# Where the sums for the output projection are made: from beside the second half of the input projection to beside the last six blocks of its first half

## The chip, the core and the metric

The kernel runs on one core of a Trainium2 chip. A core has five engines with one queue each: TensorE (PE, matrix products; PEld is its loading of stationary operands), VectorE (DVE), ScalarE (ACT), GpSimd (POOL) and SyncE (SP), which here issues nearly all transfers between the chip's memory and the core's own. The metric is the device time of one execution in microseconds. The kernel before takes 2552.73 us, the median of three runs (2552.61 to 2555.01).

## The reference

One layer of a streaming encoder on x, 2048 tokens by 1024, in fp32. Only the first part matters here:

```python
u = rms_norm(h, g_mix_pre[l])
z = u @ w_in[l]                                   # 1024 x 2816
qa, ka, va, qh, fh, ih, gh = jnp.split(z, IN_SPLITS, axis=-1)
ya = swa_with_sinks(...)                          # banded attention on qa, ka, va
yh = hgrn2(...)                                   # gated recurrence on qh, fh, ih, gh
y = jnp.concatenate([ya, yh.astype(ya.dtype)], axis=-1) @ w_out[l]    # 1024 x 1024
h = h + rms_norm(y, g_mix_post[l])
...                                               # cross-attention, then a SwiGLU FFN
```

## The kernel before

Every fp32 matrix product is made of three products in a shorter format (fp32r): an operand is split into a high part (ScalarE or GpSimd) and the rest (VectorE, the subtraction at L990).

*Blocks of seven.* Most large products use Strassen's scheme in Winograd's form. An operand is a 2 by 2 arrangement of quarters, and a product of two of them takes seven products of quarters instead of eight, at the price of sums of quarters on both sides. The stationary operand's sums are made block by block (`streamed`, L1065, whose tiles are `sraw`, `sum` and `S`). The moving operand has four sums, under the keys 5, 7, 6 and 4 (CHAIN, L992). Where the moving operand is a weight, its sums are made ahead: `combined` (L1027) loads quarters, adds or subtracts them on VectorE (L1034) and stores the results in the chip's memory. `sums` (L1418) sets aside that memory, `out_s` for the output projection's w_out, and returns a function that starts the generator `combined`. Each sum is made in two halves of 128 partitions by 1024 numbers (512 KB): eight operations, twelve quarter loads and eight stores in all. The job for the output projection reads `out_s` much later, at 778 us.

`phases` (L1219) walks through jobs of such blocks. A block of kind "s" has seven steps (STEPS, L980), each of twelve matrix products. After each step every generator in the list `after` is moved on once: the closing work of earlier blocks, and what a job's last entry names, a table from the index of a block to generators that begin at it.

*The first half of the input projection* (`in_first`, L451) is one such job over tokens 0 to 1023, with thirteen blocks: the first four are the plain halves of the first two column pairs, then come nine of kind "s", one for each further pair of column groups (ORDER, L419). The moving operand is the normalised input, the stationary one w_in. A block's results are added (L644), copied or passed through a tanh, and stored in z_d. The blocks with index 5 to 8 hold gate and query columns of the recurrence: their closing work makes the decays (`decays`, L726: logarithm, scan at L734, exponentials, with small GpSimd operations between) beside the block that follows. Also beside these blocks the second half's input is normalised, transposed (L1398) and stored. The job's table is empty, `{}`.

*The second half* (`mix`, L194) projects tokens 1024 to 2047 column by column (`in_proj`, plain products at L156 to L158) between the banded attention (`swa`, iterations with L805 to L853) and the recurrence (`hgrn`). After nine iterations the loop over the remaining eight attention iterations moves the sums' generator on by four steps each, and by one before it. There the sums use the tiles `u` (two buffers) and `x` (three buffers), which they share with the decays of this half:

```python
self.out_sums, side = self.sums("out_s", self.w_out, 4, lambda: self.io_tile("u"), lambda: self.io_tile("x"))
side = side()
next(side)
pairs = self.hgrn(range(NPB, NT), "gt")
for i, _ in enumerate(swa, NPB + 2):
    next(cols)
    ...
    for _ in range(4):
        next(side, None)
```

*What sets the order.* A planner at build time sets each engine's order: it takes instructions by the order in which the program states them, each as soon as it is ready in the planner's own reckoning of times, and it derives all waits. `behind` (L1050) keeps an operation on VectorE or ScalarE behind the last one stated before a mark, which `phases` sets after the products of each step. A tile with n buffers can be filled again when the last reader of its oldest use is done.

## Time and profile before

| what | value |
|---|---|
| median of three runs | 2552.73 us |
| the profiled execution | 2550.01 us, span 2548.3 us |
| TensorE busy | 2504.8 us (98%) |
| VectorE busy | 1792.1 us (70%) |
| ScalarE busy | 1261.6 us (50%) |
| GpSimd busy | 364.6 us (14%) |
| granted TensorE clock, mean | 0.997 |
| the eight sums (L1034 with `u` and `x`) | 448 to 524 us |
| moved by DMA | 486.33 MB, 191 GB/s over the span |

In the lines of the profile, "out<-in" names the tile that an instruction writes and those that it reads, and L with a number is the line of the kernel. A line of the order of time gives start, duration, engine, line, operation, tiles and count, and in square brackets how long the engine idled before it and what ended that. A line of the busy time by stretches gives, after the two ends of the stretch in us, its length and the busy time of PE, PEld, DVE, ACT and POOL with the number of instructions in brackets, the granted clock, the mean busy share of the 16 DMA engines, and GB/s. A line of waits gives the waiting instruction, what it waited for, the total in us, how often, and the longest. A queue's name ends in q (SPq). Products overlap in the engine, so that a product's own duration (0.39 us) is longer than the distance to the next (0.23 us).

### The profile page before, as it was taken

What the parts mean: (1) busy time and instruction counts of PE and PEld (TensorE: products, weight loads), DVE (VectorE), ACT (ScalarE), POOL (GpSimd) and SP (SyncE); (2) the same over time, 40 slices, a digit from 0 to 9 for tenths busy, and PEclk for the clock granted to TensorE, in tenths of its full rate; (3) what the DMA queues carried; (4) which work ended last, traced back from release to release, by engine and by line L of the source; (5) the groups of instructions that cost most, each with busy time, mean ns of one, the idle gap of its engine ahead of it and who ended that gap; (6) DMA issues with size and microseconds to landing.
All of it is one profiled execution on the core that took longest, in us unless ns stands there. A gap on an engine that the chain in (4) does not pass through costs nothing.

```text
span 2548.3 us, 34324 instructions
## 1 busy us (share of the span) xinstructions
PE 2504.8 (98%) x12006; PEld 2092.8 (82%) x12006; DVE 1792.1 (70%) x2871; ACT 1261.6 (50%) x2635; POOL 364.6 (14%) x540
## 2 busy tenths in 40 slices
PE   9999999999999999999999999999999999999998
PEld 8878888877997778878878888888888888878886
DVE  8885488987556989988876555576566557574766
ACT  5553466655555566566753333353333335443543
POOL 4231234321311112102200000000000000000022
PEclk9999999999999999999999999999999999999999
DMA  6455655865887996867954522254465434564786
GB/s 201 146 165 178 192 154 170 230 204 146 259 292 275 316 335 189 274 206 226 333 200 146 177 91 87 74 203 148 160 210 195 144 117 159 180 188 106 228 177 151
DMA packets 387885, 486.33 MB, mean 191 GB/s; under 512 B 22272, under 2 KB 283392, under 8 KB 387712
## 3 DMA queue, kind: packets, MB, share of 16 engines
q1 hardware_dynamic: 381664, 462.12, 55.9%
q0 software_dynamic: 6048, 22.02, 5.0%
q8 instruction: 94, 1.54, 0.2%
q14 instruction: 79, 0.65, 0.1%
HBM read 317.34 MB, written 166.72 MB: 190 GB/s over the span
## 4 chain that ended last, share of the span: by engine, by line
PE 51%; DVE 2%; DMA 1%; issue 1%; ACT 1%; POOL 0%; SPq 0%; DVEq 0%; POOLq 0%; ACTq 0%
PE psm L1133 17%; PE psm L1131 17%; PE psm L1132 17%; DVE T L990 0%; DVE S L990 0%; ACT junk L1504 0%; PE pss L1390 0%; DMA out_dram<-row 0%; DMA row<-d_s 0%; DMA row<-in_w_down_dram 0%; DMA u_d<-row 0%; DMA sraw<-in_w_gate_dram 0%; DVE sum L1106 0%; ACT S L987 0%; ACT T L987 0%
## 5 line engine op out<-in xcount | busy, mean ns | idle before, releaser
L1131 PE MATMUL psm<-T,S 128*128 128x512 f32 x2680 | 1034.1, 390 | 13.3 <-ACT part L1146 7.2
L1132 PE MATMUL psm<-T,S 128*128 128x512 f32 x2680 | 1042.3, 390 | 4.0 <-DVE T L990 3.9
L1133 PE MATMUL psm<-T,S 128*128 128x512 f32 x2680 | 1029.4, 389 | 4.1 <-DVE S L990 4.1
L1131 PEld LDWEIGHTS psm<-T,S 128*128 128x128 f32 x2680 | 503.0, 188 | 125.9 <-ACT part L1146 11.9
L1132 PEld LDWEIGHTS psm<-T,S 128*128 128x128 f32 x2680 | 503.2, 188 | 110.5 <-DVE T L990 7.3
L1133 PEld LDWEIGHTS psm<-T,S 128*128 128x128 f32 x2680 | 503.1, 188 | 110.6 <-DVE S L990 6.3
L987 ACT ACTIVATE S<-sum 128x512 fp32r<-128x512 f32 (+1 forms) x370 | 224.0, 620 | 371.5 <-PE psm L1133 267.3
L990 DVE TENSOR_TENSOR S<-sraw,S 128x512 fp32r<-128x512 f32 (+1 forms) x315 | 211.5, 679 | 218.8 <-ACT S L987 215.8
L1146 ACT ACTIVATE part<-psm 128x512 f32<-128x512 f32 x285 | 168.6, 596 | 251.9 <-PE psm L1133 230.9
L990 DVE TENSOR_TENSOR S<-sum,S 128x512 fp32r<-128x512 f32 (+1 forms) x388 | 257.4, 673 | 42.1 <-ACT S L987 38.3
L987 ACT ACTIVATE S<-sraw 128x512 fp32r<-128x512 f32 (+1 forms) x300 | 184.7, 618 | 110.8 <-PE psm L1133 106.0
L1537 POOL DMA_DIRECT2D y_d<-row x16 | 14.1, 879 | 1077.9 <-DVE row L1721 1027.6
L990 DVE TENSOR_TENSOR T<-row,T 128x1024 fp32r<-128x1024 f32 (+1 forms) x112 | 131.0, 1183 | 30.2 <-ACT T L987 29.2
L157 PE MATMUL psg<-u,whi 128*128 128x512 f32 x320 | 128.3, 401 | 0.0
L158 PE MATMUL psg<-u,wlo 128*128 128x512 f32 x320 | 127.6, 399 | 0.0
L156 PE MATMUL psg<-u,whi 128*128 128x512 f32 x320 | 127.5, 399 | 0.0
L1504 ACT ACTIVATE junk<-row 128x512 f32<-128x512 f32 x160 | 99.6, 624 | 40.6 <-DVE row L1526 20.6
L987 ACT ACTIVATE T<-row 128x1024 fp32r<-128x1024 f32 (+1 forms) x112 | 113.3, 1031 | 7.5 <-DMA row<-d_s 4.3
L1672 DVE TENSOR_TENSOR row<-psm,part 128x512 f32<-128x512 f32 x66 | 43.7, 687 | 66.9 <-PE psm L1133 66.9
L1681 DVE TENSOR_TENSOR part<-psm,part 128x512 f32<-128x512 f32 x66 | 43.8, 687 | 60.1 <-PE psm L1133 59.8
L1721 DVE TENSOR_TENSOR row<-psm,part 128x512 f32<-128x512 f32 x72 | 49.1, 688 | 49.5 <-PE psm L1133 49.4
L814 ACT ACTIVATE S<-S,w_mn 128x256 f32<-128x256 f32 (+1 forms) x128 | 63.0, 496 | 29.6 <-DVE w_mn L810 29.2
(363 smaller groups left out, 3562.2 us busy)
## 6 DMA issues: line engine op xcount, KB each, us to landing
sraw<-in_w_gate_dram SPq DMA_DIRECT2D x44, 512.0 KB, 3.6
sraw<-in_w_up_dram SPq DMA_DIRECT2D x44, 512.0 KB, 3.7
hid_d<-row SPq DMA_DIRECT2D x44, 512.0 KB, 2.7
sraw<-hid_d SPq DMA_DIRECT2D x32, 512.0 KB, 4.2
sraw<-in_w_in_dram SPq DMA_DIRECT2D x44, 256.0 KB, 4.0
z_d<-pair SPq DMA_DIRECT2D x20, 512.0 KB, 3.4
raw<-in_w_in_dram SPq DMA_DIRECT2D x20, 512.0 KB, 4.8
z_d<-z SPq DMA_DIRECT2D x20, 512.0 KB, 4.0
```

The source lines that it names most:

```text
L156: nc.tensor.matmul(ps, ah, bh, start=(i == 0), stop=False)
L157: nc.tensor.matmul(ps, ah, bl, start=False, stop=False)
L158: nc.tensor.matmul(ps, al, bh, start=False, stop=(i == n - 1))
L814: nc.scalar.activation(s[:, r, o:], s[:, r, o:], AF.Exp, bias=mn[:, i:i + 1], scale=-1.0, accum_out=den[:, i:i + 1])
L987: self.nc.scalar.activation(hi, raw, AF.Copy)
L990: self.nc.vector.tensor_tensor(lo, raw, f32(hi), ALU.subtract)
L1131: nc.tensor.matmul(ps, s[:, 0, k, :], t[:, 0, k, :], start=st, stop=False, **kw)
L1132: nc.tensor.matmul(ps, s[:, 0, k, :], t[:, 1, k, :], start=False, stop=False, **kw)
L1133: nc.tensor.matmul(ps, s[:, 1, k, :], t[:, 0, k, :], start=False, stop=sp, **kw)
L1146: nc.scalar.activation(t, ps, AF.Copy)
L1504: self.nc.scalar.activation(junk, a, AF.Square, scale=float(D) ** -0.5, accum_out=to)
L1721: nc.vector.tensor_tensor(d, a, b, ALU.add)
```

## The change

The sums of w_out for the output projection are made earlier: their generator starts at the block with index 7 of the first half's job, the eighth, and moves on once per step of the last six blocks (42 steps). It uses two tiles of its own with one buffer each, `wa` and `wb`, in the pool of that stage (`st_pool`). With `late=True` a sum is stored at the step after the one in which it is made, so that a sum takes five moves of the generator: loads, two empty ones, the operation, the store. The later loop no longer moves the sums on. For the sums that the later jobs make, `late` is False and `put` does what it did.

```diff
@@ mix
-                self.out_sums, side = self.sums("out_s", self.w_out, 4, lambda: self.io_tile("u"), lambda: self.io_tile("x"))
-                side = side()
-                next(side)
                 pairs = self.hgrn(range(NPB, NT), "gt")
                 for i, _ in enumerate(swa, NPB + 2):
                     next(cols)
                     if i == NT + 1 - 0:
                         next(pairs)
-                    for _ in range(4):
-                        next(side, None)
@@ in_first
-        phases = self.phases([(lambda i, j, a, n: raw[i, j][:, a:a + n, :], 4, blocks, None, {})], T)
+        def weight_tile(tag):
+            self._n += 1
+            return self.st_pool.tile([P, D], F32, tag=tag, name=f"{tag}_{self._n}", bufs=1)
+
+        self.out_sums, side = self.sums("out_s", self.w_out, 4, lambda: weight_tile("wa"), lambda: weight_tile("wb"),
+                                        late=True)
+        phases = self.phases([(lambda i, j, a, n: raw[i, j][:, a:a + n, :], 4, blocks, None, {7: [side]})], T)
@@ combined
-    def combined(self, get, nk, dst):
+    def combined(self, get, nk, dst, late=False):
...
                 with self.behind():
                     nc.vector.tensor_tensor(t, t, o, op)
+                if late:
+                    yield
                 self.store(dst[self.CHAIN.index(key), :, a * 512:b * 512], t.rearrange("p k d -> p (k d)"))
...
-                    put(4, o, t, ALU.subtract)
+                    yield from put(4, o, t, ALU.subtract)
                 else:
-                    put(key, t, o, ALU.add if key == 6 else ALU.subtract)
+                    yield from put(key, t, o, ALU.add if key == 6 else ALU.subtract)
                 yield
@@ sums
-    def sums(self, name, src, nk, *tiles):
+    def sums(self, name, src, nk, *tiles, late=False):
...
-        return dst, lambda: self.combined(get, nk, dst)
+        return dst, lambda: self.combined(get, nk, dst, late)
```

## The prediction

> **What bounds the kernel now.** I read the page first, then the busy time by stretches of 25 us over the two stages that the change touches, then what TensorE waited for in them, and last the order of time on VectorE and on the DMA queue.
>
> ```profile
> PE 2504.8 (98%) x12006; PEld 2092.8 (82%) x12006; DVE 1792.1 (70%) x2871; ACT 1261.6 (50%) x2635; POOL 364.6 (14%) x540
> ```
>
> TensorE is busy for 2504.8 of 2548.3 us, so all its idle time together is 43.5 us. The change removes no matmul. It can only move this idle time, and 0.2% of the time is 5.1 us. The stretches say where it lies.
>
> ```profile
> core 0: us, PE busy (x) PEld busy (x) DVE busy (x) ACT busy (x) POOL busy (x), PEclk, DMA share, GB/s
> 100.00:125.00 25.00, 24.50 (x108) 19.97 (x107) 22.74 (x31) 15.61 (x25) 10.50 (x13) 1.00 0.41 127
> 125.00:150.00 25.00, 22.85 (x100) 18.29 (x99) 23.71 (x31) 17.31 (x26) 11.50 (x13) 1.00 0.48 143
> 150.00:175.00 25.00, 24.05 (x106) 19.58 (x105) 23.66 (x32) 13.50 (x22) 11.59 (x14) 1.00 0.50 152
> 175.00:200.00 25.00, 25.00 (x112) 20.70 (x111) 14.88 (x23) 8.26 (x15) 2.69 (x5) 1.00 0.69 226
> 200.00:225.00 25.00, 25.00 (x112) 20.69 (x111) 15.29 (x23) 8.42 (x14) 2.76 (x4) 1.00 0.50 174
> 275.00:300.00 25.00, 23.85 (x124) 19.91 (x123) 17.91 (x57) 12.95 (x45) 7.80 (x13) 0.93 0.75 203
> 475.00:500.00 25.00, 24.90 (x138) 20.95 (x136) 23.43 (x45) 16.60 (x46) 8.81 (x14) 1.00 1.08 289
> 500.00:525.00 25.00, 23.83 (x124) 19.42 (x123) 21.72 (x54) 13.53 (x38) 7.39 (x9) 1.00 1.04 321
> 525.00:550.00 25.00, 24.27 (x122) 19.60 (x122) 21.80 (x62) 13.94 (x43) 8.04 (x13) 1.00 0.61 189
> 625.00:650.00 25.00, 22.27 (x170) 21.16 (x168) 18.15 (x25) 15.38 (x31) 4.65 (x7) 0.93 0.95 256
> ```
>
> The sums now run in the stage from 445 to 525 us, where VectorE is busy 87 to 94% and TensorE idles 0.10, 1.17 and 0.73 us in the three stretches shown. The first half of the input projection is two stages in one: up to 175 us VectorE is busy 23.7 of 25 us and TensorE loses 0.50, 2.15 and 0.95 us; from 175 us VectorE has 10 us of each 25 to spare and TensorE loses nothing.
>
> Where block eight begins follows from the decays, which are made beside the block after theirs. Their eight scans are four pairs on VectorE from 106.10 to 167.98 us, beside the blocks with index 6, 7, 8 and 9, so one of these blocks takes 61.88/3, 20.6 us. Block eight (index 7) begins near 125 us, index 8 near 146, index 9 near 166, and the last ends near 246.
>
> ```profile
> L734 DVE TENSOR_TENSOR_SCAN pair<-reset,pair x8: 1192/1208/1562, 106.1 to 169.1; 128x512 f32<-128x512 f32 x8
> PE psm L1131 <- ACT part L1146: 4.1, 5, 1.2
> 148.99 0.50 PE L1131 MATMUL psm<-T,S 128*128 128x512 f32 x1 [1.20 <-ACT part L1146]
> 157.66 1.48 DVE L672 SCALAR_TENSOR_TENSOR pair<-pair,pair 128x512 f32<-128x512 f32 x2 [0.31 <-ACT pair L749]
> 159.83 1.22 DVE L754 SCALAR_TENSOR_TENSOR pair<-pair,pair 128x1024 f32<-128x1024 f32 x1 [0.69 <-ACT pair L750]
> 160.97 1.28 DVE L644 TENSOR_TENSOR pair<-psm,part 128x512 f32<-128x512 f32 x2
> 162.17 0.68 DVE L990 TENSOR_TENSOR S<-sum,S 128x512 fp32r<-128x512 f32 x1
> 167.41 0.64 DVE L990 TENSOR_TENSOR S<-sum,S 128x512 fp32r<-128x512 f32 x1
> 167.98 1.21 DVE L734 TENSOR_TENSOR_SCAN pair<-reset,pair 128x512 f32<-128x512 f32 x1
> ```
>
> In these blocks TensorE waits once a block, about 1.2 us, for a copy on ScalarE that releases a bank. That copy stands behind the decays' logarithm, which stands behind what VectorE delivers at 160.97. VectorE works without a gap from there to the next scan, and its only idle time in the loop is 0.31 and 0.69 us. So the loop from scan to scan is VectorE's, and what is put into it lengthens the block.
>
> **The change part by part.** *The operations that move.* Eight sums leave the later stage and come into the first half, at these prices now:
>
> ```profile
> L1034 DVE TENSOR_TENSOR u<-u,x x6: 1198/1214/1224, 448.1 to 521.9; 128x1024 f32<-128x1024 f32 x6
> L1034 DVE TENSOR_TENSOR x<-x,u x2: 1206/1216/1225, 494.4 to 523.6; 128x1024 f32<-128x1024 f32 x2
>   DMA out_s<-u: 2.8, 1
>   issue: 0.3, 1
> 521.91 1.22 DVE L1034 TENSOR_TENSOR u<-u,x 128x1024 f32<-128x1024 f32 x1 [2.76 <-DMA out_s<-u]
> 523.05 0.68 DVE L853 TENSOR_TENSOR ys<-psh,ys 64x512 f32<-64x512 f32 x1
> PE psh L805 <- DVE ys L853: 0.7, 1, 0.7
> ```
>
> One is 1.21 us, all eight 9.7 us. In the new place a sum takes five steps of the generator: loads, two idle steps, the operation at the fourth, the store at the fifth. The generator moves once per step, seven steps a block, 42 steps in the six blocks from index 7; 41 are needed, so all fit. The operations fall on steps 4, 9, 14, 19, 24, 29, 34 and 39. That is one in block index 7, two in index 8, and five in index 9 to 12.
>
> *Cost of the three early operations.* The first comes just ahead of the row at L672, where VectorE idles 0.31 us: it costs 1.21 less 0.31, 0.9 us. The second comes between the scan and what follows it, with no gap: 1.2 us. The third comes at the end of index 8, ahead of the scan at 168 us. It delays that, but the block after it is the last with decays, and TensorE waits for nothing in 175 to 225 us: between 0 and 1.2, I take 0.6. Sum 2.7 us, bounds 0.9 (first alone counts) and 3.6 (three in full).
>
> *Cost of the five late operations.* Nothing: 5 times 1.21 is 6.1 us over some 75 us in which VectorE idles 10 of every 25. If that cover were gone they would cost up to 6.1.
>
> *Waits of these operations for their data.* In the stage before, eight operations waited 2.8 and 0.3 us, 0.38 each on average, and TensorE felt it: the 2.76 us wait held L853, and TensorE waited 0.7 us for L853. Behind a sum that waits now stand the additions at L644, the decays and the splits, whose readers are ScalarE and TensorE. For the three early ones I take 3 times 0.38, 1.1 us; bounds 0 and 3 times 2.76, 8.3 us. The five late ones wait in VectorE's spare time.
>
> *The DMA queue.* SP receives 20 load commands for twelve tiles (those of the upper half of rows are two commands each) and eight stores, in a stage where the DMA share is 0.41 to 0.69; it loses them in a stage at 1.04 to 1.08. The tiles are now one buffer each. So three loads (steps 6, 21 and 26) wait for the landing of the store issued one step earlier, and the third and seventh operations for a store four steps earlier.
>
> ```profile
> L78 SPq DMA_DIRECT2D out_s<-u x6: 326/334/543, 449.3 to 523.2; - x6
> L78 SPq DMA_DIRECT2D out_s<-x x2: 320/429/538, 496.8 to 524.9; - x2
> DMA to landing us min/median/max: 2.6/6.0/10.9
> 198.62 0.92 SPq L75 DMA_DIRECT2D sraw<-in_w_in_dram  x2
> 208.90 0.68 DVE L1106 TENSOR_TENSOR sum<-sraw,sraw 128x512 f32<-128x512 f32 x1
> sraw<-in_w_in_dram SPq DMA_DIRECT2D x44, 256.0 KB, 4.0
> ```
>
> The landing line covers all accesses of the sums' array (eight stores and eight later loads), median 6.0 us. A step is 20.6/7, 2.9 us. So SP stands about 3.1 us at each such load, and behind it stand the weight loads of the next block (sraw), loads of x and stores of z. These have cover: the weights issued at 198.62 land about 4.0 us later and are first read at 208.90, 6.3 us to spare. I take 0 for it. If the cover is gone it is at most 3 times 3.1, 9.3 us.
>
> The Trainium skill, DMA: Bandwidth & Descriptors, section on the anatomy of a DMA, fits a transfer by 2.0 us plus its bytes over 436 GB/s, for the software path. By it 512 KB would land in about 3.2 us (an estimate), SP would stand 0.3 us instead of 3.1, and the sum would be the same, with 0.9 in place of 9.3 as its far end. The row's median of 6.0 us comes from a stage with a full DMA, so the true one may lie between.
>
> *What the later stage gains.* VectorE loses 9.7 us of work and 3.1 us of waits between 445 and 525 us. TensorE's idle time there is the upper bound on the gain: 0.10 plus 1.17, and 0.73 more until 550 us if the lag is carried on. Below it is 0. I take 1.3 us, since these waits, with the one for L853 above, are for VectorE:
>
> ```profile
> PE pss L839 <- DVE w_mn L810: 0.5, 1, 0.5
> PE psh L849 <- DVE ptl L844: 0.3, 1, 0.3
> ```
>
> *Hand-over between the stages.* Two tiles of 4 KB per partition are added to the pool of the first half, and the next stage's tiles come to lie elsewhere. The stretch 275 to 300 us has the granted clock at 0.93, 7% of 25 us or 1.7 us. A shift of the work may add one such stretch or remove one; I take 0, ends minus 1.7 and 1.7.
>
> *Sum.* 2.7 + 1.1 - 1.3 = +2.5 us on the profiled execution's 2550.0 us (span 2548.3), so 2552.5. That execution is 2.7 us under the median of the runs, 2552.73; on the median the forecast is 2555.2 us, 0.10% slower, which lies inside the 0.2% (5.1 us) that a measurement of this kernel can tell from no change.
>
> **The rivals.** *Slower: the sums wait in VectorE's full stretch.* The mechanism is the wait of 2.76 us above, now at all three early operations. For it: the buffers are single, and the loads for a sum are issued only three steps (8.7 us) ahead, with SP standing up to 3.1 us of that. Against it: VectorE lags there, which gives the loads time. It gives 2.7 + 8.3 - 1.3, +9.7 us, 2562.4. It decides the sign of the measurement once the waits exceed 3.7 us in total (2.7 + 3.7 - 1.3 = 5.1), which is two of three.
>
> The Trainium skill, TensorE: Matmul & The Clock Gate, part 1, says that the clock falls to half after an idle window of about 3.4 us; a stall of that length would add about 1.7 us to this rival, by an estimate from the page. This trace has the clock at 0.93 in 275 to 300 us with 1.15 us of idle time in the whole stretch, so less idle time is enough here.
>
> *Slower: SP's queue holds the weights.* A load that stands for the landing of a store holds the next block's weights past the 6.3 us of cover, and the stationary operands are late. It needs landings near the 10.9 maximum: 10.9 - 2.9 - 6.3, 1.7 us of stall each, at three places 5.1 us; +7.6 us with the sum above, 2560.3.
>
> *Faster.* The later stage is freed of more than its own waits: all 2.0 us of 475 to 550, and the hand-over in 625 to 650 us with its 2.73 us idle and 1.7 us of low clock, while only the first early operation costs its 0.9: -5.5 us, 2547.2. For it speaks that VectorE is full up to 550 us. Against it: the last sum ends at 525, and the longest wait of the hand-over is for a load.
>
> ```profile
> PE pst L902 <- DMA v<-z_d: 2.6, 1, 2.6
> ```
>
> **How the numbers follow.** I give the forecast (2555.2, within 0.2%) 0.48, the slower rivals 0.30 and 0.08, the faster one 0.14. The likeliest case's own range is 2550 to 2558: the ends 0.9 - 2.0 - 1.7 = -2.8 and +5.1. The range for all reaches to the faster rival's 2547 and just past the slower ones' 2562.4, to 2563; about 2 in 10 is left out, most of it waits with a low clock on top and gains beyond the rival's. Faster 0.14, same 0.48, slower 0.38.
>
> **What would show it.** Right: the sums' rows on VectorE stand near 135, 150, 165 us and later, each 1.2 us; TensorE's wait for the copy at L1146 near 149 and 168 us grows from 1.2 to about 2 us; from 175 to 246 us TensorE idles as little as now; the whole first half ends 2 to 4 us later; the idle time of the stretches from 475 to 525 us (shifted by as much) falls below 0.3 us. Wrong: a wait for a landing ahead of a sum of over 1 us at two places (the slower rival), splits waiting for sraw (the second), scans still 20.6 us apart in spite of the sums (then the loop has slack that I don't see), or a later stage that becomes shorter by more than 2 us.

## The result and the profile after

The kernel after takes 2563.07 us, the median of six runs (2561.36 to 2565.05), beside 2552.85 us for the kernel before in the same comparison (2552.24 to 2555.01). That is 10.2 us more, a ratio of 1.004 with a 95% interval of 1.003 to 1.005. In a second comparison the ratio was 1.003 (1.0015 to 1.0045). The change makes the kernel slower by 0.3 to 0.4%. The forecast was +0.10%, and the end of the range, 2563, was just missed.

In the kernel after, lines 238 to 535 have numbers smaller by five, and those from 537 on numbers larger by one to three: the products are L1134 to L1136 (before L1131 to L1133), the copy that releases a bank L1149 (L1146), the addition L645 (L644), the scan L735 (L734), the sums L1035 (L1034).

Line of the page on the busy time of the engines, kernel after (span 2561.5 us, the execution itself 2563.24 us):

```profile
PE 2508.2 (98%) x12006; PEld 2098.1 (82%) x12006; DVE 1794.0 (70%) x2871; ACT 1260.1 (49%) x2635; POOL 363.3 (14%) x540
```

The work is the same, so the time is TensorE's idle time and its clock. Busy time by stretches, kernel before and then kernel after (columns: the stretch, its length, PE, PEld, DVE, ACT, POOL with their instructions, granted clock, DMA share, GB/s):

```profile
25.00:50.00 25.00, 24.88 (x136) 21.18 (x136) 23.75 (x33) 12.97 (x25) 14.94 (x17) 1.00 0.51 151
100.00:250.00 150.00, 145.91 (x638) 119.19 (x637) 116.40 (x159) 75.00 (x116) 42.38 (x54) 1.00 0.50 157
475.00:550.00 75.00, 73.00 (x381) 59.96 (x380) 66.94 (x159) 44.07 (x126) 24.23 (x35) 1.00 0.91 266
600.00:700.00 100.00, 94.74 (x686) 88.23 (x685) 57.22 (x96) 53.67 (x135) 24.99 (x34) 0.98 0.74 217
```

```profile
25.00:50.00 25.00, 21.63 (x120) 18.00 (x119) 18.84 (x27) 10.53 (x22) 14.97 (x17) 1.00 0.63 148
100.00:250.00 150.00, 142.44 (x622) 116.03 (x621) 123.87 (x163) 76.11 (x118) 46.60 (x55) 1.00 0.68 217
475.00:550.00 75.00, 74.30 (x401) 62.71 (x399) 66.81 (x173) 47.32 (x135) 24.83 (x38) 1.00 0.48 153
600.00:700.00 100.00, 92.77 (x636) 86.56 (x637) 50.74 (x78) 46.35 (x112) 20.53 (x27) 0.95 0.72 213
```

The two kernels differ at four places. TensorE loses 3.25 us more between 25 and 50 us, a place that the prediction does not speak of. It loses 3.5 us more between 100 and 250 us. Between 475 and 550 us it loses 1.3 us less. Between 600 and 700 us it is busy 2 us less and its clock is 0.95 instead of 0.98, worth another 3 us of work; the prediction has this place only in its faster rival, as a gain.

Since the stretches shift against each other, the exact account is made at equal work: the products in TensorE's order are given their undisturbed spacing (0.227 us for 512 columns and so on), and two traces are compared by the time at which the same sum of spacings is reached. This lag is my working from the start times of the 12006 products; the spacing taken for the smaller products moves a term by up to 0.6 us. The table gives what each stretch (named by the times of the kernel before) adds to the lag behind the profiled execution before, in us. Each row is one execution of the kernel named. The last column is the difference of the medians.

| kernel | to 57 | 57–272 | 272–316 | 316–479 | 479–563 | 563–625 | 625–672 | 672–941 | rest | sum | medians |
|---|---|---|---|---|---|---|---|---|---|---|---|
| after | +3.8 | +4.1 | −2.6 | −0.1 | −2.8 | −0.1 | +5.7 | +3.2 | +2.1 | +13.2 | +10.2 |
| after_again | +4.3 | +4.6 | −2.1 | +0.4 | −2.8 | −0.1 | +4.0 | +6.6 | −0.8 | +14.1 | +8.9 |
| before_again | −0.5 | +0.9 | 0.0 | +0.1 | +0.1 | 0.0 | −1.3 | +0.7 | +1.1 | +1.2 | |
| early_loads_alone | +3.2 | +1.8 | −2.3 | +0.3 | −0.7 | 0.0 | +1.5 | +2.3 | +1.4 | +7.5 | +2.7 |
| held_loads | −0.5 | +9.5 | −2.3 | +0.1 | −2.8 | −0.1 | +3.5 | +1.9 | +0.1 | +9.3 | +9.7 |
| held_behind_x | −0.2 | +8.1 | −2.0 | +0.8 | −2.8 | −0.1 | +4.6 | +7.4 | +2.8 | +18.5 | +9.8 |
| small_ops | −0.1 | +5.8 | −2.8 | +1.1 | −2.8 | −0.1 | +2.9 | +5.4 | −1.3 | +7.9 | +3.6 |
| from_nine | 0.0 | +5.8 | +4.2 | +0.3 | −2.8 | −0.1 | +3.3 | +3.8 | −0.4 | +14.1 | +8.8 |
| not_late | +5.2 | +8.7 | −2.2 | +0.8 | −2.8 | −0.2 | +4.0 | +6.1 | +0.5 | +20.2 | +10.2 |
| held_next | +4.9 | +2.8 | −1.8 | +0.3 | −2.8 | +0.5 | +5.5 | +2.0 | +0.4 | +11.9 | +7.7 |
| both | +3.8 | +4.4 | −0.3 | +0.8 | +1.9 | 0.0 | −0.3 | +3.2 | +9.2 | +22.8 | +17.0 |
| in_fold | −0.1 | −0.1 | −2.1 | +0.8 | −2.7 | −0.1 | +8.0 | +3.4 | −1.0 | +6.0 | +2.1 |
| old_late | −0.4 | +0.3 | −2.6 | 0.0 | −0.1 | 0.0 | −0.1 | +4.3 | +3.1 | +4.5 | −0.7 |
| first_nine | −0.3 | +0.3 | +5.2 | +5.7 | −4.0 | +1.0 | +2.5 | +3.1 | −0.9 | +12.6 | +8.7 |
| spread | −0.3 | −0.3 | +4.0 | +4.2 | −2.1 | −0.3 | +5.0 | +4.7 | −0.1 | +14.8 | +7.3 |

The profiled execution before is 2.7 us under its median, which is why most sums lie above the differences of the medians. The stretches 272 to 316, 672 to 941 and the rest vary by several us between kernels that are alike there: old_late, whose median is that of the kernel before, has −2.6, +4.3 and +3.1 in them. So nothing is read from these three in the kernel after. The other terms are +3.8, +4.1, −0.1, −2.8, −0.1 and +5.7, together +10.6 us against +10.2 measured; the three left out add up to +2.7, as much as the execution before lay under its median, a match that may be chance.

**The start.** Order of time on the queue of SP, kernel after:

```profile
18.14 1.71 SPq L75 DMA_DIRECT2D wa<-in_w_out_dram  x2
19.89 0.61 SPq L75 DMA_DIRECT2D wb<-in_w_out_dram  x1
21.02 3.41 SPq L75 DMA_DIRECT2D sraw<-in_w_in_dram  x2
24.47 0.61 SPq L75 DMA_DIRECT2D wb<-in_w_out_dram  x1
25.18 4.61 SPq L75 DMA_DIRECT2D sraw<-in_w_in_dram  x4
```

The loads of the first two quarters (four commands, 1 MB) are stated at the block with index 7, near 125 us, but they are issued at 18 us. They depend on nothing, their tiles are free from the start, and the planner takes each instruction as soon as it is ready. In the kernel before eight loads of the first weights (sraw) stand at that place:

```profile
18.26 9.86 SPq L75 DMA_DIRECT2D sraw<-in_w_in_dram  x8
```

Now they come later, and the DMA share from 25 to 50 us is 0.63 instead of 0.51. Who waited on GpSimd between 18 and 50 us, before and then after (total, times, longest in us):

```profile
POOL S_u L989 <- DMA sraw<-in_w_in_dram: 0.8, 1, 0.8
```

```profile
POOL S_u L990 <- DMA sraw<-in_w_in_dram: 5.3, 3, 4.3
```

In the same stretch, from 25 to 50 us, TensorE waited 3.4 us in the kernel after, 2.1 of them for a split on VectorE (L991); in the kernel before it idles 0.1 us there.

**The first half.** Waits of TensorE from 100 to 250 us, kernel after (total, times, longest in us):

```profile
PE psm L1134 <- ACT part L1149: 6.7, 5, 2.0
PE psm L1134 <- DVE pair L645: 0.8, 1, 0.8
```

One line of its order of time there:

```profile
154.95 0.50 PE L1134 MATMUL psm<-T,S 128*128 128x512 f32 x1 [2.05 <-ACT part L1149]
```

The wait for the copy is the one of before (4.1 us in five), grown by 2.6 us. Of this growth 1.0 us stands at 113 and 134 us, ahead of the first sum, and after_again does not have it. The other 1.7 us stands at 155 and 176 us, where the first two sums are in VectorE's order: 2.05 and 1.78 us, where the kernel before has 1.20 and 0.95 (after_again 1.92 and 1.67). The order of time on VectorE, kernel after, the three early sums and the sixth with the addition behind it:

```profile
140.40 1.22 DVE L1035 TENSOR_TENSOR wa<-wa,wb 128x1024 f32<-128x1024 f32 x1
153.08 1.59 DVE L1035 TENSOR_TENSOR wa<-wa,wb 128x1024 f32<-128x1024 f32 x1
178.17 1.21 DVE L1035 TENSOR_TENSOR wa<-wa,wb 128x1024 f32<-128x1024 f32 x1
210.01 1.23 DVE L1035 TENSOR_TENSOR wa<-wa,wb 128x1024 f32<-128x1024 f32 x1 [6.23 <-DMA wa<-in_w_out_dram]
211.16 1.28 DVE L645 TENSOR_TENSOR pair<-psm,part 128x512 f32<-128x512 f32 x2
```

The scans stand as one group (first and last start):

```profile
L735 DVE TENSOR_TENSOR_SCAN pair<-reset,pair x8: 1192/1210/1560, 111.1 to 175.5; 128x512 f32<-128x512 f32 x8
```

From the first scan to the last it is now 64.4 us, where it was 63.0. The early sums have no bracket: they waited for nothing. The third came at 178 us, behind the last scan and not ahead of it. The one at 210 us waited 6.2 us for its load, and the addition L645 stood behind it, for which TensorE then waited 0.8 us (2.8 in after_again). The queue of SP shows why that load was late: its tile has one buffer, so it went out only when the store of the sum before, in the same tile, had landed (3.3 us after its issue), and it then took 6.6 us itself.

```profile
200.08 0.32 SPq L78 DMA_DIRECT2D out_s<-wa  x1
203.44 0.37 SPq L75 DMA_DIRECT2D wa<-in_w_out_dram  x1
```

**The hand-over.** Waits of TensorE from 610 to 680 us, kernel after; before, the longest was the one for a load of `v` in the prediction:

```profile
PE pst L926 <- ACT vt L905: 4.5, 2, 2.5
PE psg L887 <- DVE z L714: 2.4, 1, 2.4
```

ScalarE's order of time shows what stood in front. The splits of the output projection's first operands (`T<-z`) waited there for their loads, and the copies for which TensorE waited stood behind them: the last column's `z` at 631.11 us, and `vt`.

```profile
629.20 1.06 ACT L988 ACTIVATE T<-z 128x1024 fp32r<-128x1024 f32 x1 [5.90 <-DMA z<-in_w_out_dram]
636.50 1.06 ACT L988 ACTIVATE T<-z 128x1024 fp32r<-128x1024 f32 x1 [2.86 <-DMA z<-in_w_out_dram]
637.46 0.58 ACT L905 ACTIVATE vt<-pst 128x512 f32<-128x512 f32 x1
```

first_nine and, but for held_next, all executions with the sums in the first half alone have these two waits, 3.2 to 5.5 us for `vt` and 1.8 to 2.6 us for `z`. Part of the loss is clock. The granted clock is at half for 10.2 us in this stretch of the kernel after, for 3.4 us in after_again and in the kernel before, and not at all in before_again. So 3.4 of the +5.7 us in the table are clock in the one execution, and none of the +4.0 in the other.

### The profile page after: what moved, and what is told of

It is laid out like the page before. It is cut to its first block, busy times and chain, and to the rows that moved or that the text cites. A ratio compares the mean times of both kernels' runs of the same rounds, so it can differ in the third digit from the quotient of the medians.

```text
span 2561.5 us, 34342 instructions
## 1 busy us (share of the span) xinstructions
PE 2508.2 (98%) x12006; PEld 2098.1 (82%) x12006; DVE 1794.0 (70%) x2871; ACT 1260.1 (49%) x2635; POOL 363.3 (14%) x540
## 4 chain that ended last, share of the span: by engine, by line
PE 57%; DVE 3%; DMA 3%; issue 1%; ACT 1%; SPq 0%; POOL 0%; DVEq 0%; POOLq 0%; ACTq 0%
PE psm L1136 19%; PE psm L1135 19%; PE psm L1134 19%; DVE T L991 1%; DVE S L991 1%; DMA sraw<-in_w_gate_dram 0%; ACT junk L1507 0%; PE pss L1393 0%; DVE sum L1109 0%; DMA row<-qk_s 0%; DVE row L1401 0%; DMA h1t_d<-row 0%; DMA row<-qk_d 0%; DMA row<-in_w_down_dram 0%; DMA row<-vo_s 0%
## 5 line engine op out<-in xcount | busy, mean ns | idle before, releaser
L1134 PE MATMUL psm<-T,S 128*128 128x512 f32 x2680 | 1035.8, 391 | 18.3 <-ACT part L1149 10.0
L1136 PE MATMUL psm<-T,S 128*128 128x512 f32 x2680 | 1032.2, 391 | 4.4 <-DVE S L991 4.2
L1134 PEld LDWEIGHTS psm<-T,S 128*128 128x128 f32 x2680 | 504.0, 188 | 131.2 <-ACT part L1149 14.7
L1136 PEld LDWEIGHTS psm<-T,S 128*128 128x128 f32 x2680 | 504.4, 188 | 111.4 <-DVE S L991 7.3
L991 DVE TENSOR_TENSOR S<-sraw,S 128x512 fp32r<-128x512 f32 (+1 forms) x315 | 211.9, 682 | 208.2 <-ACT S L988 206.6
L1149 ACT ACTIVATE part<-psm 128x512 f32<-128x512 f32 x285 | 168.6, 596 | 252.1 <-PE psm L1136 231.5
L991 DVE TENSOR_TENSOR S<-sum,S 128x512 fp32r<-128x512 f32 (+1 forms) x388 | 259.9, 681 | 40.7 <-ACT S L988 38.7
L991 DVE TENSOR_TENSOR T<-row,T 128x1024 fp32r<-128x1024 f32 (+1 forms) x112 | 131.3, 1186 | 30.6 <-ACT T L988 28.6
L1109 DVE TENSOR_TENSOR sum<-sraw,sraw 128x512 f32<-128x512 f32 (+1 forms) x97 | 66.3, 683 | 15.9 <-issue 9.3
```

The lines of the kernel that those rows point to most:

```text
L991: self.nc.vector.tensor_tensor(lo, raw, f32(hi), ALU.subtract)
L1109: nc.vector.tensor_tensor(t, a, b, op)
L1134: nc.tensor.matmul(ps, s[:, 0, k, :], t[:, 0, k, :], start=st, stop=False, **kw)
L1136: nc.tensor.matmul(ps, s[:, 1, k, :], t[:, 0, k, :], start=False, stop=sp, **kw)
L1149: nc.scalar.activation(t, ps, AF.Copy)
```

## The experiments

**Only the early loads.** To the kernel before, a generator at the block with index 7 adds the loads of the first two quarters into `wa` and `wb`, which nothing reads; the sums stay in the second half.

```diff
+        def fetched():
+            for tag, i, j in (("wa", 0, 1), ("wb", 0, 0)):
...
+                self.w_out(t.rearrange("p (k d) -> p k d", d=512), i, j, 0, 2)
+            yield
-        ... blocks, None, {})], T)
+        ... blocks, None, {7: [fetched]})], T)
```

> The kernel before, with only two tiles of 4 KB and the four load commands that the change's first sum begins with, stated at the same place (block with index 7); nothing reads them. The sums stay where they were. Theory early loads: the planner puts these commands near 18 us as in the changed kernel, TensorE loses 3.4 us between 25 and 50 us, and the time is 2552.9 + 3 to 4, about 2556.5. Rival: the loads are harmless and the time is that of the kernel before within 1 us.

2557.74 us, +2.7, ratio 1.001 (1.0 to 1.0019). Busy time by stretches:

```profile
25.00:50.00 25.00, 22.20 (x122) 18.45 (x122) 19.45 (x27) 10.47 (x22) 14.96 (x17) 1.00 0.62 154
```

TensorE is busy 2.7 us less from 25 to 50 us, with no sum anywhere near. So the loss at the start (+3.2 of the +3.8) is shown to come with the four load commands issued at 18 us and their two tiles. The runs that follow keep the tiles and hold the loads back, and there it is gone, so the loads are its cause.

**Holding the loads back.** `queued` keeps what is stated in it behind a given instruction in the planner's order. held_loads ties the first loads to SP's sixth command from the last, held_behind_x to its last one, the load of x stated just before (`[-1]` in place of `[-6]`). held_no_ops is held_loads without the eight operations. small_ops is held_behind_x with each operation on one number per partition.

```diff
+        hold = []
+        if late:
+            hold = [[i for i in nc.cur_bb.bb.instructions if i.engine == mybir.EngineType.SP][-6]]
...
-                if x:
-                    t = get(0, *x, a, b - a)
-                o = get(1, *y, a, b - a)
+                with self.queued(*hold):
+                    if x:
+                        t = get(0, *x, a, b - a)
+                    o = get(1, *y, a, b - a)
+                hold = []
```

> The changed kernel with one edit: the four load commands for the first sum's two tiles may be issued only after the DMA command that the program states six before them. In the changed kernel they stand at 18 us, among the first loads of x and w_in, and TensorE loses 3.8 us between 30 and 45 us. Theory early loads: that loss is theirs; TensorE idles 0.1 us instead of 3.4 us from 25 to 50 us, and the time falls by 3 to 4 us, to about 2559.5. Rival VectorE alone: the sums in the full blocks are the whole cause, the loss at the start has another origin, and the time stays at 2563 within 1 us.

> The changed kernel with the first sum's loads issued behind the load of x that block index 7 states (with held loads they stood just ahead of a load of x at 94 us, which then landed 7.0 us after its issue, and ScalarE waited 5.3 us for it). Theory: a load of x just behind the sums' loads comes late and stops ScalarE, and through it TensorE. Then neither the loss at 30 to 45 us (3.8) nor that at 107 us (6.0) appears, and the first half ends 4 us sooner than in the changed kernel, near 251 us; time about 2559. Rival: any place for these loads costs as much, 2563.

> The previous kernel without the eight operations on VectorE (the loads and stores stay, so the sums are left out and what is stored is a quarter of w_out or an earlier one). Theory VectorE loop: the operations in the blocks from 125 to 175 us cost TensorE about 3 us there, so the first half ends 3 us sooner than with held loads and the time is about 2556. Rival DMA: the loads and stores themselves hold the stage up, then the first half is no shorter, and the time stays within 1 us of the run with held loads.

> The previous kernel, each of the eight operations cut to one column of 128 numbers (so the stored sums are left undone but for that column); loads, stores, waits and their order stay. Theory VectorE loop: the waits at the copy near 128, 149 and 170 us fall back by 0.3, 0.9 and 0.8 us to those of the kernel before, and the first half ends 2 us sooner than with full operations. Rival DMA: these waits come from loads that are late, and stay.

held_loads takes 2564.74 us, ratio 1.0041 (1.0028 to 1.0053); held_behind_x 2564.17, 1.0039 (1.0024 to 1.0054); held_no_ops 2572.2, 1.0072 (1.0057 to 1.0087); small_ops 2557.96, a single run. The hold does what it says: the loss at the start is gone in all four (−0.5 to, in held_no_ops, +0.9). But nothing is gained, because 57 to 272 us now costs 8.1 to 9.5 us instead of 4.1. In held_loads the loads go out at 88.70 us, and the load of x issued at 93.73 us is late behind them (order of time on ScalarE):

```profile
100.70 1.06 ACT L424 ACTIVATE pair<-pair 128x1024 f32<-128x1024 f32 x1 [5.32 <-DMA pair<-in_x_dram]
```

The copy that releases TensorE's bank stood behind this instruction in ScalarE's order, and TensorE waited 3.8 us for it, until 110.9 us. In held_behind_x the load of x goes out just ahead, at 113.48 us, and the four loads from 114.03 us on; it still took 8.1 us to land instead of 4.7, with a wait of 2.8 us on ScalarE. So 1 MB of loads next to a load of x had a price at both places, in front of it and behind it. Part of the price is clock: in held_loads the granted clock is 0.86 from 100 to 125 us, in held_behind_x 0.93 from 125 to 150 and from 150 to 175 us, some 3.5 us of work in either, and 1.00 throughout in the kernel after. held_no_ops was meant to show the price of the operations and does not: without them the loads and stores depend on so little that the planner moved most to 90 to 150 us, and TensorE waited 7.0 us until 115.6 us. Its +16.3 us is of another order, not of the operations' absence. small_ops keeps the order but for the second sum, which comes behind the scans at 151 us instead of ahead of them. From 57 to 272 us it loses 5.8 where held_behind_x loses 8.1. Of these 2.3 us 1.7 stand near 206 us, where the sixth sum waited 2.7 us for its load instead of 5.9, and only 0.5 by 182 us. Its waits for the copy at the first two sums are 1.1 and 2.1 us, together as long as in held_behind_x (2.0 and 1.3), so the expected fall of both did not come. What the operations' own time costs is therefore not shown; the two executions differ in the transfers as well.

**Starting two blocks later.** The generator starts at index 9, past the blocks with decays, held behind the load of x, and moves on by 2, 1, 2, 1 per step so that all fit.

```diff
-        ... blocks, None, {7: [side]})], T)
+        ... blocks, None, {9: [lambda: uneven(side())]})], T)
```

> As held behind x, but the sums begin at the block with index 9 and the generator moves 2, 1, 2, 1 times a step, so that all eight operations fall where VectorE has 10 of 25 us to spare. Theory VectorE loop: the blocks up to 175 us take as long as in the kernel before, and the first half ends within 2 us of the kernel before (246 us); time about 2553 to 2556, what is left being waits for landings (loads only one and a half steps, 4 us, ahead of an operation). Rival: the transfers in this stretch (DMA share 1.00 in the changed kernel) delay weights and sums, the first half ends 5 us or more after 246.

2563.23 us, ratio 1.0036 (1.0022 to 1.005). Up to 182 us the lag is 1.3 us, so the loop of the decays is spared. By 252 us it is 5.8, and 4.2 us more come at 272 to 286 us, where TensorE waits 2.7 us for a load of `vr` and the clock falls for 6.8 us. VectorE's spare time after 175 us did thus not cover the sums in this run, whose loads come only one and a half steps ahead of an operation: eight of them there cost 5.8 us up to 272 us, against 4.1 and 4.6 in the kernel after.

**The late store.** old_late stores each sum one step later at the old place (five moves per iteration); not_late is the kernel after with `late=False`.

```diff
-                                        late=True)
+                                        late=False)
```

> The kernel before with one part of the change alone: at the old place each sum is stored one step later than it is made (five moves of the generator per iteration, for four). If the later store matters, the 2.8 us wait of a sum for a store near 520 us changes; either theory expects the time within 2 us of the kernel before.

> The changed kernel with each sum stored in the step in which it is made (the other part of the change alone). The loads at 18 us stay, so the 3.8 us at the start stay; the sums follow each other in four steps for five, so one more falls before 175 us. Theory VectorE loop: 0 to 2 us slower than the changed kernel, or the same. Rival: the later store holds up the tiles, then it is faster, by the 6 us wait for wa near 205 us at most.

old_late takes 2554.27 us, ratio 1.0 (0.999 to 1.001). not_late takes 2565.23, ratio 1.005 (1.0031 to 1.0069), beside 1.004 (1.003 to 1.005) with the late store. At the old place it changes nothing; at the new one the intervals overlap. No effect of it is seen, so it does not explain the slower kernel.

**The sums in both places, and in the hand-over.** both is the kernel after plus the old sums at their old place, into a second array that nothing reads. in_fold is the kernel before with the generator moved on in the loop after the attention, the hand-over itself, with two tiles `u`.

```diff
+                _, side = self.sums("out_t", self.w_out, 4, lambda: self.io_tile("u"), lambda: self.io_tile("x"))
+                side = side()
+                next(side)
...
+                    for _ in range(4):
+                        next(side, None)
```

> The changed kernel, with the old sums made at their old place as well (into memory that nothing reads). In the changed kernels with the sums gone from the second half, TensorE loses 3 to 5 us more than before between 620 and 670 us. Theory vacated place: that loss comes because VectorE, freed of the sums, takes up work of the next stage whose loads are not there; then with the old sums back it is gone, and so is the 2.5 us gain near 500 us, so the time is near that of the changed kernel, 2561 to 2564. Rival first half: the loss at 620 to 670 us follows from the longer first half, and stays; then the time is 2565 to 2567.

> The kernel before with the sums taken out of the second half and made later, beside the folding of the cross-attention weights (625 to 770 us), where VectorE is busy 10 to 16 of 25 us. The first half is that of the kernel before. Theory vacated place: the loss of 3 to 5 us at 620 to 670 us appears here too, with the gain of 2.5 us near 500 us; time 2553 to 2557. Rival first half: no such loss; the gain stands and the time is 2550 to 2552.

both takes 2572.03 us, ratio 1.0068 (1.0048 to 1.0089); in_fold 2557.11, 1.0012 (1.0003 to 1.0021). Busy time by stretches, both:

```profile
475.00:550.00 75.00, 71.38 (x376) 58.31 (x375) 63.72 (x147) 40.66 (x111) 24.92 (x33) 1.00 0.86 253
600.00:700.00 100.00, 94.41 (x661) 87.49 (x660) 59.95 (x109) 52.90 (x130) 20.75 (x30) 0.98 0.69 203
```

With the sums back at the old place, the loss at 479 to 563 us is back too, and the one at 625 to 672 us is gone (−0.3), although the first half is that of the kernel after. So the hand-over does not lose because of what comes in the first half. But both lies 17.0 us behind the kernel before, 6.8 more than the kernel after, outside what either theory expected: it loses 4.7 us more at 479 to 563, and 7.1 more after 941 us, far from either place, for which I have no cause. in_fold, busy time by stretches:

```profile
100.00:250.00 150.00, 146.04 (x639) 119.28 (x638) 116.34 (x159) 74.94 (x116) 41.65 (x53) 1.00 0.50 157
475.00:550.00 75.00, 74.29 (x395) 62.46 (x394) 64.25 (x166) 47.95 (x140) 20.95 (x36) 1.00 0.47 148
600.00:700.00 100.00, 89.04 (x627) 83.84 (x627) 53.41 (x73) 45.28 (x105) 26.50 (x28) 0.95 0.92 249
```

Here the first half is untouched (146.04 us busy, as before), the later stage gains its 2.7 us, and the hand-over loses 8.0, partly its own sums.

**A hand-over that starts later.** Between the last column of the projection and the recurrence, `queued` holds the next stage's work behind the last instruction on ScalarE and VectorE: in the kernel after (held_next), before (before_held_next) and in_fold (fold_held).

```diff
+                last = [self.traced(getattr(mybir.EngineType, e)) for e in ("Activation", "DVE")]
+                with self.queued(*last):
+                    for _ in range(2):
+                        next(fold)
...
+                        with self.queued(*last):
+                            next(phases)
```

> The changed kernel with one edit in the second half: the operations on ScalarE and VectorE of the stage after it (the folded cross-attention weights, the splits of the output projection's first operands) are queued behind the last operation of the last column. Theory vacated place: TensorE's waits for z at L714 (2.4 us near 631) and for vt (2.5 and 1.9 us near 635 and 660) shrink to under 1 us each, the loss from 600 to 675 us falls from 5.6 to under 2 us, the time to about 2559. Rival: these waits come from loads that are late whatever the order, and the time stays at 2563.

> The same edit on the kernel before, as the control: there the last column's operation does not wait behind the next stage's (its wait at 628 us is for a load of v). Theory vacated place: no gain, 2553 to 2557. If it gains as much as on the changed kernel, the edit helps by itself and shows nothing of the change.

> The sums beside the folding of the weights (as in_fold), with the same edit. First half as before, gain of 2.5 us near 520 us kept. Theory vacated place: the 8 us lost from 620 to 675 us in in_fold fall to under 4, time 2549 to 2553, at or under the kernel before. Rival: the sums' own loads and operations cost that stretch, and the time stays at 2555 to 2558.

held_next takes 2561.86 us, ratio 1.0028 (1.0017 to 1.004); before_held_next 2557.14, 1.0007 (0.9997 to 1.0017); fold_held 2571.35, 1.006 (1.0042 to 1.0079). In held_next the waits for `vt` and `z` are gone, and others of the same size stand in their place (waits of TensorE from 610 to 680 us):

```profile
PE pss L156 <- ACT whi L991: 3.8, 1, 3.8
PE psg L947 <- ACT atz L892: 1.9, 1, 1.9
```

The loss there stays at +5.5. So holding the next stage's work back takes the two waits away and does not give the loss back. The control, before_held_next, cannot be told from the kernel before. fold_held loses some 8 us at 625 to 672 us and some 18 at 672 to 941; why is open.

**The sums where TensorE idles nothing.** first_nine takes the kernel before and moves the generator on beside the first nine attention iterations instead of the last eight (its sums ran from 256.6 to 415.5 us). spread moves it on by two steps instead of four in this loop and in the one after it, so that half of the sums stay.

```diff
+                self.out_sums, side = self.sums("out_s", self.w_out, 4, lambda: self.io_tile("u"), lambda: self.io_tile("x"))
+                side = side()
+                next(side)
                 for _ in range(NPB + 1):
                     next(swa)
                     next(hgrn)
                     next(cols)
+                    for _ in range(4):
+                        next(side, None)
```

> The kernel before with the sums moved on beside the first nine attention iterations of the second half, from the start of that loop (about 290 to 415 us), with the same tiles u and x; the first half is untouched. Beside these iterations TensorE is busy for all of every 25 us and VectorE for 18 to 22.5. Theory V (taking the sums out of the stretch from 450 to 525 us is what makes the hand-over at 600 to 700 us slower): TensorE loses nothing near the sums, gains 2.5 us from 480 to 545 and loses 4 to 5.6 from 600 to 675: +1.5 to +3 us, and the last attention result stands 10 us or more ahead of the last column. Theory L (the hand-over is slower because of what the first half does to the order or the lag): only the gain of 2.5 us stays, -2.5 us, and the last attention result stands about 3 us ahead of the last column, as before.

> The kernel before with the sums moved on by two steps instead of four beside each of the seventeen attention iterations, from the start of the first loop. Half of the sums stay beside the last eight iterations. Theory V: about half of each effect, -1.2 us from 480 to 545 and +2 to +2.8 at the hand-over, about +1 us in all. Theory L: -1 to -2.5 us.

first_nine takes 2563.19 us, ratio 1.0042 (1.0029 to 1.0056); spread 2561.88, 1.0031 (1.002 to 1.0043). Busy time by stretches, first_nine:

```profile
250.00:300.00 50.00, 45.31 (x212) 37.90 (x211) 18.11 (x44) 11.88 (x37) 13.64 (x21) 0.93 1.09 280
400.00:475.00 75.00, 72.17 (x423) 62.17 (x423) 65.27 (x144) 50.49 (x145) 29.40 (x45) 1.00 0.55 166
475.00:550.00 75.00, 75.00 (x406) 63.78 (x405) 62.83 (x168) 48.03 (x134) 23.92 (x38) 1.00 0.49 153
600.00:700.00 100.00, 90.74 (x644) 83.86 (x643) 56.01 (x91) 48.93 (x118) 21.22 (x29) 1.00 0.69 202
```

With the first half untouched, the vacated stage gains (75.00 of 75 busy, −4.0 by the lag) and the hand-over loses 2.5 to 3.5, so theory V holds in its direction. Its other half, that the sums cost nothing beside a TensorE without idle time, did not come out: 10.9 us are lost from 272 to 479 us. But it was not tested alone, since the loads did not stay there. Nine load commands of the sums go out from 245.01 us, ahead of the attention's first loads. `qq` is issued at 267.88 us instead of 260.18, GpSimd could begin on it at 276.35 instead of 263.57, and TensorE waited 3.3 us for the result (kernel first_nine, orders of time on SP and GpSimd, then TensorE's wait):

```profile
245.01 1.70 SPq L75 DMA_DIRECT2D u<-in_w_out_dram  x2
276.35 0.61 POOL L879 TENSOR_TENSOR qq<-qq,G 128x256 f32<-128x256 f32 x1 [14.03 <-DMA qq<-z_d]
```

```profile
PE psh L886 <- POOL qq L879: 3.3, 1, 3.3
```

This is the loss at the start of the kernel after once more, at the start of another stage: 5.2 of the 10.9 us stand at 272 to 316 us, with the clock at 0.93 instead of 0.97 from 250 to 300 us. The other 5.7 stand beside the iterations. No run holds these loads back, so the price of the sums themselves there is open.

Theory V also says how: that without the sums the attention ends well ahead of the projection's last column, which leaves less beside it. The last results of the attention (`ys`) and of the columns (`z`) on VectorE, in the kernels before, after and spread (count, minimum, median and longest in ns, first and last start in us):

```profile
L853 DVE TENSOR_TENSOR ys<-psh,ys x9: 673/694/695, 562.4 to 624.7; 64x512 f32<-64x512 f32 x9
L713 DVE SCALAR_TENSOR_TENSOR z<-z,psg x8: 670/678/689, 569.7 to 627.5; 128x512 f32<-128x512 f32 x8
```

```profile
L854 DVE TENSOR_TENSOR ys<-psh,ys x8: 669/686/694, 569.1 to 617.9; 64x512 f32<-64x512 f32 x8
L714 DVE SCALAR_TENSOR_TENSOR z<-z,psg x8: 664/680/689, 572.8 to 632.6; 128x512 f32<-128x512 f32 x8
```

```profile
L855 DVE TENSOR_TENSOR ys<-psh,ys x12: 671/688/695, 544.3 to 630.1; 64x512 f32<-64x512 f32 x12
L715 DVE SCALAR_TENSOR_TENSOR z<-z,psg x8: 666/676/689, 574.1 to 632.6; 128x512 f32<-128x512 f32 x8
```

The distance is 2.8 us before, 14.7 after and 14.1 in first_nine (623.5 and 637.6), but 2.5 in spread, which loses 5.0 at the hand-over all the same. So the distance is not the mechanism. What stands is the split by executions at 625 to 672 us. The eleven that lack all or half of the sums at the old place and have none in the hand-over (those of the table, and held_no_ops with +5.5) lose 2.5 to 5.7 us, 4.2 on average. The five that have all of them there (before_again, old_late, both, early_loads_alone, and before_held_next with −0.2) lie between −1.3 and +1.5, −0.1 on average. The way from the one to the other is open: the loads of `z` for which ScalarE waited go out at 623.70 us in the kernel after and at 616.97 in the kernel before, and no run shows what puts them later.

after_again and before_again are the two kernels unchanged:

> The changed kernel once more, for its profile. What belongs to its order of instructions comes again: TensorE's loss of 3.4 us from 25 to 50 us, the waits at the copy L1149 near 111, 132, 153 and 174 us, the wait at 625 to 650 us. What was chance of one execution (low clock at 905 and 977 us, 3.4 us each) does not. Time 2563 within 1.5 us.

> The kernel before once more, for its profile. If its first profile is typical, the hand-over after the first half has low clock near 290 us again, the one near 641 us too, and TensorE's loss between 620 and 660 us and between 840 and 900 us is as before (each within 1 us). If the first profile was a lucky one, these stretches lose 2 to 5 us more, and that part of the difference between the two kernels is not of the change.

They gave 2563.91 us, ratio 1.003 (1.0015 to 1.0045), and 2551.23 us, a single run. Their rows in the table show how far the terms repeat: within 0.9 us up to 316 us, within 0.1 at 479 to 563, within 1.7 at 625 to 672, and within 3.4 beyond. The low clock of the first profile at 631 us did not come again in before_again. No version that I ran is faster than the kernel before.

## Why the prediction was right or wrong

The forecast of 2555.2 us, no measurable change, was wrong by 7.9 us. The slower rival's 2562.4 is close to the result, but its mechanism, waits of 2.76 us at the three early operations, did not happen: their rows show no wait. Its nearness is luck.

- *Three early operations, +2.7, and their waits, +1.1.* Too large together, and wrong in the split. The wait for the copy grew at the first two sums as stated, to about 2 us, which is +1.7 us in the kernel after and +1.4 in after_again. The third sum fell behind the last scan and cost nothing that the lag shows, and the waits for data were nil. That the operations' own time makes this growth is argued from VectorE's order; small_ops does not confirm it.
- *Five late operations, 0.* Failed. The idle time of VectorE did not cover a wait of 6.2 us at 210 us, since what stands behind the waiting sum is needed by TensorE: +1.1 us by the lag in the kernel after, +3.1 in after_again. The prediction had named both parts of this, the load that waits for the landing of a store (step 26) and the addition L644 behind a waiting sum, and had not put them together for the late ones. from_nine, with all eight in that place, lost 4.5 us there.
- *The DMA queue, 0.* This step failed most clearly. It took the loads to be issued where the program states them and asked only what stands behind them there. The first four were issued at 18 us among the first loads of the weights, +3.8 us, and early_loads_alone with the runs that hold them back shows them to be the cause. The description of the kernel before says that the planner takes an instruction as soon as it is ready; by that, tiles that nothing used before are ready from the start. The rival on SP's queue comes nearest, weights that are late behind other loads, but it had them at another place and behind the landing of a store.
- *How fast a store lands.* The row's 6.0 us was too long for this stage, and for the old one too: it mixes stores with later loads, and the eight stores alone landed in 2.6, 4.2 and 6.6 us there (minimum, median, maximum, kernel before). In the kernel after, all stores of `out_s` in the first half landed in 2.6, 3.5 and 10.8 us (in the same order):

```profile
DMA to landing us min/median/max: 2.6/3.5/10.8
```

  The 3.2 us, the prediction's estimate from the Trainium skill, DMA: Bandwidth & Descriptors, section on the anatomy of a DMA, is nearer to this median than the row of the full stage was; it does not give the 10.8.
- *The later stage, −1.3 (0 to −2.0).* Right in kind, too small: −2.8 us, beyond the end taken, in every execution with the sums in the first half alone. A gain of over 2 us was one of the prediction's own signs of being wrong.
- *The hand-over at 600 to 700 us, no term.* Failed: +5.7 us in the kernel after, +4.0 in after_again. The prediction's own term for a hand-over, 0 (±1.7), is that at 275 to 300 us, from which nothing is read here. For the later one it let the gain of the vacated stage stand and had a change there only in its faster rival, as a gain. In the nine executions with the sums in the first half alone, taking them out of the second half gains 2.8 us and costs 2.9 to 5.7 at the hand-over. With the first half untouched it is 4.0 against 2.5 (3.5 with the stretch before it) in first_nine and 2.1 against 5.0 in spread.

Summed, the forecast's +2.5 became +10.6 by +3.8 (loads at the start), +0.3 (first half: 4.1 against 3.8), −1.5 (later stage) and +5.7 (hand-over), less the two small terms of 0.1. That the first half came out so near is luck: its 4.1 us are 1.7 at the early sums, 1.1 behind the late one, and 1.3 ahead of the first sum, which after_again does not have.

## What to carry to other kernels

Where a planner or scheduler sets the order, a moved load is not where the program states it: ask what the load depends on, and if the answer is nothing, count it at the start of the kernel, in front of the first loads on which everything waits. An engine's spare time covers an operation only if the operation does not wait, because everything behind it in the engine's order waits with it. And a stage that is freed of work is not free of consequences: cost the next stage's start as well, since what ran beside the work now meets other work.

## What the runs showed of the hardware

The granted clock falls after little idle time, and not every time. In the kernel before, stretches of 4 us:

```profile
275.00:279.00 4.00, 2.85 (x17) 1.99 (x16) 3.97 (x5) 1.56 (x5) 2.00 (x2) 1.00 0.30 89
279.00:283.00 4.00, 4.00 (x14) 3.20 (x14) 3.67 (x21) 3.49 (x16) 0.41 (x2) 0.57 0.85 270
```

TensorE idles 1.15 us in the first, and the longest single gap there is 0.85 us; the clock is then 0.57 for 4 us. The Trainium skill, TensorE: Matmul & The Clock Gate, part 1, gives an idle window of about 3.4 us as the condition; here much less sufficed. The low stretch lasts 3.4 us at half clock (0.57 over 4 us), which is the length of the window on that page. The kernel after has 0.16 and 0.65 us of idle time at the same place and keeps its full clock:

```profile
280.00:284.00 4.00, 3.84 (x22) 3.29 (x20) 1.99 (x3) 1.75 (x3) 2.43 (x3) 1.00 0.21 59
284.00:288.00 4.00, 3.35 (x21) 2.99 (x22) 4.00 (x17) 2.04 (x10) 0.50 (x2) 1.00 0.73 228
```

Some 1.7 us of a term can come and go in this way, as in the stretch 272 to 316 us of the table. Other loads next to a load lengthen it: the load of x at 113 us landed in 4.7 us in the kernel before and in 8.1 us in held_behind_x, with 1 MB of weights issued right behind it.
